# Layer 1's mixers: column tiles projected as three products of split operands, with four buffers of projected tiles

## The chip, the core and the metric

The kernel runs on one core of a Trainium2 chip. Its time is the device time of one execution in microseconds (us). A core has engines that work side by side, each on its own instructions in order: TensorE (PE; its weight loads are listed as PEld), VectorE (DVE), ScalarE (ACT), GpSimd (POOL) and SyncE (SP), whose queue issues most DMA transfers. A wait of one for another goes through semaphores.

## The reference

Two layers of a backbone with 256 latent tokens and 256 context tokens of width 1024. In each layer a modulated norm is multiplied by one input matrix, whose columns go to four mixers, and their outputs by one output matrix; then comes an expert layer. Cut to what matters here:

```python
for l in range(DEPTH):                      # DEPTH = 2
    need_ctx = l < DEPTH - 1
    h  = rms_norm(x,   norm1_g[l]) * (1 + sc1)  + sh1
    hc = rms_norm(ctx, norm1_g[l]) * (1 + csc1) + csh1
    P  = split(h  @ w_in[l]); Pc = split(hc @ w_in[l])
    y_a = conv_mixer(P[0:3]); y_b, yc_b = rwkv_mixer(P[3:9], Pc[3:9], need_ctx)
    y_c = attention(P[9:12], Pc[9:12]); y_d, yc_d = mlstm_mixer(P[12:17], Pc[12:17], need_ctx)
    x = x + gt1 * (concat(y_a, y_b, y_c, y_d) @ w_out[l])
    x = x + gt2 * peer_ffn(rms_norm(x, norm2_g[l]) * (1 + sc2) + sh2)
    if need_ctx: ...                        # the same for ctx, in layer 0 alone
```

In layer 1 the context is read but not updated: of its columns only those are wanted that feed the recurrence's state, the attention's keys and values and the mLSTM's state.

## The kernel before

Everything lies transposed: channels on the 128 partitions, the 256 tokens along the free axis. The input matrix is cut into 26 column tiles of 128; a pair of them makes one projected tile `pj` of 128 x 2 x 256. The program passes through five phases, each with its own pools of buffers: layer 0's context mixers, layer 0's latent mixers, layer 0's experts, layer 1's mixers (context first, then latents), layer 1's experts.

`mixers` (from L1070 on) is one function for all. It makes the modulated norm h (`modnorm`), and `project` then multiplies pairs of column tiles: gates and k, v, r, then the recurrence (rwkv, names rw), then keys, values and queries and the attention (at), then q, k, v, o and the mLSTM (ml), then the three tiles of the convolution (cv), and at last the output projection (wo) with the four results y. Layer 1's context takes 6 of the 13 pairs, its latents all 13. A name such as ps_p_pj1l is the PSUM bank of a projection in layer 1, latents; pj1c is layer 1, context; pj0c and wo0c are layer 0's context.

`proj` (L356) has two forms. In the native form a weight tile is loaded in halves of 128 x 512 float32 (wraw) and multiplied as it is with h (hfull): one product for each of 8 slices of the channels, which TensorE runs as two instructions. In the split form `load_split` (L333) has ScalarE copy the weights to a rounded high part (whi, type fp32r) and VectorE subtract it from the weights for a low part (wlo); h has a high and a low part likewise (hhi, hlo), and each slice takes three products: high times high, low times high, high times low. In `native` (the tuple NAT, for the phases of layer 0's context and of layer 1) it is chosen: layer 0's context phase is split, with three buffers of raw halves and two of each part (WBA = 3, 2), layer 1's phase is native, with six raw halves (WBD = 6, 0). The projected tiles have 6, 4 and 6 buffers in the three phases (PJ).

Beside them run the ada blocks: twelve for each layer, which make the modulation vectors from the conditioning; a block is eight matmuls of 32 x 512 on weights that a DMA brings each time (araw, 256 KB), a copy and four small matmuls with sel. Eight of layer 1's blocks stand in the mixers' phase of layer 1.

The order of the instructions on each engine is not written out: a scheduler makes it when the program is built, from the data's dependencies, from priorities in the order of the code, and from which buffers are free by its own estimate of times. A projected tile's buffer can be used again as soon as its last reader is done, whichever tile it was. Once built, each engine runs its list strictly in that order.

Of the kernel before, what the change touches and what calls it, by code (L numbers as in the profile page):

```python
# [24 lines left out]
DEPTH = 2  # L25
N2 = 2
YY = 6, 7, 1
NAT = False, True
HB = 1
BA = {"p": 2, "r": 3, "x": 2, "a": 1}  # L30
BD = {"p": 2, "r": 3, "x": 2, "a": 1}
ZA = "a", "a"
ZD = "a", "a"
A0 = 32
PJ = 6, 4, 6
RB = (8, 13, 4)
NW = None, None
NL = 4
LD = {"k": 2, "g": 3, "a": 1}, {"k": 3, "g": 1}
HN = 'cv', 'at', 'ml', 'rw'  # L40
WBA = 3, 2
WBD = 6, 0
XX = 7, 8, 1
CV = 0, 1, 0, 0
PA = 6, 2, 0, 0
# [179 lines left out]
class Gen:  # L225
# [1215 lines left out]
    def run(self):  # L1441
# [5 lines left out]
        with self.pool("kp") as self.kp:  # L1447
            with self.phase(MB, dict(MS, r=AR, pj=PJ[0]), {"y": "x"}, wb=WBA, native=NAT[0]) as self.ps, self.pool("wp") as self.wp:
                with self.pool("ap") as self.ap:
# [19 lines left out]
            with self.tc.using_default_side("right"):  # L1469
                self.gp = right.enter_context(self.pool("gp"))  # L1470
            with self.phase({"p": 2, "r": 4, "m": 2}, {"p": (1, 2), "r": RB, "m": (4, 3), "pj": PJ[1], "rw_gm": 4, "rw_gn": 1},
                            {"x": "r", "y": "r"}, (4, 0), True) as self.ps, self.pool("wp") as self.wp, self.pool("mp") as self.mp, self.pool("rp") as self.rp:
# [13 lines left out]
        with self.pool("kp") as self.kp:  # L1486
            with self.phase(BD, dict(MS, x=XX, y=YY, r=RR, pj=PJ[2]), {} if "y" in BD else {"y": "x"}, wb=WBD, native=NAT[1]) as self.ps, self.pool("wp") as self.wp, self.pool("mp") as self.mp:
                self.aa = *ZD, "araw"
# [65 lines left out]
```

## Time and profile before

| what | us |
| --- | --- |
| median of 3 runs | 3282.89 (3269.38 to 3284.17) |
| the profiled execution | 3267.95 |
| its span | 3266.2 |
| layer 0's context mixers in it | 40 to 357 |
| layer 0's latent mixers, with the context's expert routing | 357 to 688 |
| layer 1's mixers | 1961 to 2386 |
| layer 1's experts | from 2386 on |

The page gives busy time by engine, the chain of work that ended last, the costliest groups of instructions and the DMA issues. A TensorE instruction's span covers its way through the array, so spans of neighbours overlap: its busy time says when something was in flight, and the pitch of instructions, start to start, says how fast it works. A wait is idle time of an engine ahead of an instruction, with what ended it.

### The profile page before, as it was taken

To read this page: it belongs to the slowest core of one execution; us is meant where nothing else is said; L and a number is where in the kernel's file an instruction comes from. 1 tells how busy PE (TensorE), PEld (TensorE's weight loads), DVE (VectorE), ACT (ScalarE), POOL (GpSimd) and SP (SyncE) were. 2 spreads that over 40 slices of the span, in tenths; PEclk is the share of its full clock that TensorE was granted. 3 is DMA by queue.
4 is the path that set the end of the run, shared out by engine and by line. 5 is a ranking of instruction groups with operands and counts; after the bars stand their busy time and mean duration, and the time that the engine had idled before them with its cause. 6 is when DMAs were issued, how large, how long until landed. Compare 5 with 4: busy or idle time off the path is not lost.

```text
span 3266.2 us, 47313 instructions
## 1 busy us (share of the span) xinstructions
PE 3104.0 (95%) x18135; PEld 2630.5 (81%) x18135; DVE 2113.9 (65%) x4700; ACT 1287.7 (39%) x1752; POOL 435.3 (13%) x370
## 2 busy tenths in 40 slices
PE   7998998979989999999999999999999899999999
PEld 5576886758878989999979987867688678999998
DVE  3655476489977777777777766475368665555554
ACT  4324414235553333333333334242233554444443
POOL 0100010000014334333333320010000000000000
PEclk9899999989999999999999999999999999999999
DMA  7333412245678888887887753232344586666663
GB/s 248 123 103 121 131 51 68 84 137 197 228 284 301 295 300 283 299 294 283 283 294 284 288 196 100 69 108 74 106 166 148 223 279 210 215 205 208 213 213 129
DMA packets 278642, 640.30 MB, mean 196 GB/s; under 512 B 22672, under 2 KB 111888, under 8 KB 272912
## 3 DMA queue, kind: packets, MB, share of 16 engines
q1 hardware_dynamic: 238960, 498.66, 45.0%
q0 software_dynamic: 36864, 134.23, 11.7%
q10 hardware_dynamic: 2592, 4.39, 0.4%
q8 instruction: 142, 2.33, 0.3%
q14 instruction: 84, 0.69, 0.1%
HBM read 591.06 MB, written 46.14 MB: 195 GB/s over the span
## 4 chain that ended last, share of the span: by engine, by line
PE 72%; DVE 8%; issue 7%; ACT 6%; DMA 4%; POOL 2%; ACTq 0%; SPq 0%; DVEq 0%; POOLq 0%
PE ps_acc_ex L289 21%; PE ps_u_ex L289 19%; PE ps_a_ada L289 3%; ACT G L294 3%; PE ps_p_pj1l L289 2%; PE ps_r_rw0c L289 2%; PE ps_u_ey L289 2%; POOL ga_row L1406 2%; PE ps_p_pj0l L289 2%; PE ps_p_pj0c L289 2%; PE ps_g_gm L289 2%; PE ps_r_rw1l L289 2%; PE ps_r_rw0l L289 2%; PE ps_k_wq1l L289 2%; ACT L294 1%
## 5 line engine op out<-in xcount | busy, mean ns | idle before, releaser
L297 DVE TENSOR_TENSOR wlo<-wraw,whi 128x1024 fp32r<-128x1024 f32 (+1 forms) x560 | 648.6, 1160 | 504.7 <-ACT whi L294 502.4
L294 ACT ACTIVATE whi<-wraw 128x1024 fp32r<-128x1024 f32 (+1 forms) x560 | 563.4, 1007 | 861.2 <-PE ps_u_ex L289 452.9
L289 PE MATMUL ps_u_ex<-hhi,wlo 128*128 128x384 f32 (+1 forms) x1632 | 509.5, 312 | 0.0
L289 PE MATMUL ps_u_ex<-hhi,whi 128*128 128x384 f32 (+1 forms) x1632 | 509.0, 312 | 0.0
L289 PE MATMUL ps_u_ex<-hlo,whi 128*128 128x384 f32 (+1 forms) x1632 | 508.5, 312 | 0.0
L289 PE MATMUL ps_acc_ex<-whi,pe_ahi 128*128 128x512 f32 x1280 | 397.6, 392 | 13.0 <-ACT pe_ahi L294 13.0
L289 PE MATMUL ps_acc_ex<-wlo,pe_ahi 128*128 128x512 f32 x1280 | 397.9, 392 | 12.7 <-DVE wlo L297 12.7
L289 PE MATMUL ps_acc_ex<-whi,pe_alo 128*128 128x512 f32 x1280 | 396.9, 391 | 0.0
L289 PEld LDWEIGHTS ps_u_ex<-hhi,whi 128*128 128x128 f32 x1632 | 309.4, 190 | 5.9
L289 PEld LDWEIGHTS ps_u_ex<-hlo,whi 128*128 128x128 f32 x1632 | 309.3, 190 | 5.9
L289 PEld LDWEIGHTS ps_u_ex<-hhi,wlo 128*128 128x128 f32 x1632 | 309.2, 189 | 0.1
L289 PEld LDWEIGHTS ps_acc_ex<-wlo,pe_ahi 128*128 128x128 f32 x1280 | 240.2, 188 | 68.4 <-DVE wlo L297 16.4
L289 PEld LDWEIGHTS ps_acc_ex<-whi,pe_alo 128*128 128x128 f32 x1280 | 241.0, 188 | 52.0
L289 PEld LDWEIGHTS ps_acc_ex<-whi,pe_ahi 128*128 128x128 f32 x1280 | 236.5, 189 | 53.6 <-issue 13.3
L1406 POOL DMA_INDIRECT ga_row<-in_u,ga_i x128 | 187.6, 1466 | 409.7 <-DVE ga_a L1414 277.4
L1406 POOL DMA_INDIRECT ga_row<-in_v,ga_i x128 | 172.3, 1346 | 319.6 <-DVE ga_acc L304 291.6
L294 ACT ACTIVATE pe_ahi<-pe_a 128x384 fp32r<-128x384 f32 (+1 forms) x192 | 106.5, 556 | 235.1 <-DVE pe_a L297 163.8
L294 ACT ACTIVATE G<-ps_g_gm 128x512 f32<-128x512 f32 x160 | 158.7, 1076 | 78.9 <-PE ps_g_gm L289 78.3
L304 DVE SCALAR_TENSOR_TENSOR ga_acc<-ga_row,ga_a,ga_acc 128x1024 f32<-128x1024 f32 x127 | 163.1, 1285 | 4.3 <-DMA ga_row<-in_v,ga_i 2.3
L297 DVE TENSOR_TENSOR pe_alo<-pe_a,pe_ahi 128x384 fp32r<-128x384 f32 (+1 forms) x192 | 115.1, 600 | 77.4 <-ACT pe_ahi L294 77.3
L1414 DVE CUSTOM_DVE_ANT_0 ga_junk<-ga_row,ga_tok 128x1024 bf16<-128x1024 f32 x128 | 156.3, 1221 | 6.3 <-DMA ga_row<-in_u,ga_i 4.6
L289 PE MATMUL ps_u_ex<-hfull,xraw 128*128 128x256 f32 x576 | 143.8, 391 | 6.2 <-DVE hfull L301 6.2
(793 smaller groups left out, 4911.5 us busy)
## 6 DMA issues: line engine op xcount, KB each, us to landing
wraw<-in_v SPq DMA_DIRECT2D x256, 512.0 KB
wraw<-in_u SPq DMA_DIRECT2D x204, 512.0 KB
araw<-in_ada SPq DMA_DIRECT2D x192, 256.0 KB
wraw<-in_win SPq DMA_DIRECT2D x180, 256.0 KB
gd<-G SPq DMA_DIRECT2D x40, 1024.0 KB
xraw<-in_u SPq DMA_DIRECT2D x52, 512.0 KB
G<-gd SPq DMA_DIRECT2D x16, 1536.0 KB
wraw<-in_wq SPq DMA_DIRECT2D x32, 512.0 KB
```

What stands on the lines that cost most here:

```text
L289: self.nc.tensor.matmul(out, lhsT, rhs, start=start, stop=stop, skip_group_check=True)
L294: self.nc.scalar.activation(out, in_, func, bias=bias, scale=scale, **kw)
L297: return (eng or self.nc.vector).tensor_tensor(out=out, in0=a, in1=b, op=op)
L304: self.nc.vector.scalar_tensor_tensor(out=out, in0=a, scalar=s, in1=b, op0=op0, op1=op1)
L1406: nc.gpsimd.indirect_dma_start(out=row, out_offset=None, in_=self.I[tab], in_offset=bass.IndirectOffsetOnAxis(ap=ei[:, n : n + 1], axis=0))
L1414: nc.vector.tensor_tensor_reduce(out=junk, in0=row, in1=tok, scale=1.0, scalar=0.0, op0=ALU.mult, op1=ALU.add, accum_out=a[:, n : n + 1])
```

## The change

Three numbers change, and all for layer 1's mixers:

```diff
-NAT = False, True
+NAT = False, False
-PJ = 6, 4, 6
+PJ = 6, 4, 4
-WBD = 6, 0
+WBD = 3, 2
```

With native False, `proj` takes the split form for all column tiles and the output matrix, `parts` gives hhi and hlo in place of hfull, `modnorm` makes h in slices of 128 x 512 and splits each, and `mixers` splits y before the output projection. There are three raw halves and two of each part in place of six raw halves, and four projected tiles in place of six. The operands' bytes from memory stay the same. All that follows for the order comes from the scheduler.

TensorE at the beginning of the phase, before: ps_a_ada is an ada block, ps_p_pj1c the context's projections, ps_r_rw1c the context's recurrence.

```order
L289 MATMUL ps_p_ex_16925<-sq,ones 128x256 x8
L289 MATMUL ps_a_ada_17699<-araw,cvs 32x512 x6
L289 MATMUL ps_p_pj1c<-hfull,wraw 128x256 x48
L289 MATMUL ps_r_rw1c<-hn_sq,const 128x512
L541 MATMUL ps_r_rw1c<-const,pj_v 128x128 x4
```

And of the change, there:

```order
L289 MATMUL ps_a_ada_17856<-araw,cvs 32x512 x6
L289 MATMUL ps_p_pj1c<-hhi,whi 128x256
L289 MATMUL ps_a_ada_17856<-araw,cvs 32x512
L289 MATMUL ps_p_pj1c<-hlo,whi 128x256
L289 MATMUL ps_p_pj1c<-hhi,wlo 128x256
L289 MATMUL ps_p_pj1c<-hhi,whi 128x256
L289 MATMUL ps_p_pj1c<-hlo,whi 128x256
L289 MATMUL ps_p_pj1c<-hhi,wlo 128x256
```

Each native product has become a group of three, and the rest of the ada block, which stood behind 48 products, now stands among the first ones; until the context's recurrence starts there are 1.4 ada blocks instead of 0.5, and until that of the latents 4.4 instead of 1.4.

VectorE in the latents' recurrence, before, where the second direction's small steps (rw_row and rw_T, eight columns more at each step) alternate with the merge of the first one (rw_X) and the attention:

```order
L297 TENSOR_TENSOR rw_row_18372<-rw_row_18372,rw_M_18363 128x8x2
L820 STREAM_SHUFFLE at_sw<-at_tmp 128x256
L297 TENSOR_TENSOR rw_T_18364<-rw_T_18364,rw_row_18372 128x8x2
L297 TENSOR_TENSOR at_q<-at_tmp,exact 128x256
L700 STREAM_SHUFFLE rw_row_18372<-rw_T_18364 128x8x3
L297 TENSOR_TENSOR ps_x_at1l<-ps_x_at1l,mask 128x128
L297 TENSOR_TENSOR rw_row_18372<-rw_row_18372,rw_M_18363 128x8x3
```

And of the change, at the same steps:

```order
L297 TENSOR_TENSOR rw_row_18878<-rw_row_18878,rw_M_18869 128x8x2
L297 TENSOR_TENSOR wlo<-wraw,whi 128x512
L297 TENSOR_TENSOR rw_T_18870<-rw_T_18870,rw_row_18878 128x8x2
L297 TENSOR_TENSOR at_q<-at_q,at_sw 128x256
L700 STREAM_SHUFFLE rw_row_18878<-rw_T_18870 128x8x3
L297 TENSOR_TENSOR rw_X<-ps_r_rw1l,mask 128x16x16
L297 TENSOR_TENSOR rw_row_18878<-rw_row_18878,rw_M_18869 128x8x3
L297 TENSOR_TENSOR wlo<-wraw,whi 128x512
```

Subtractions for weights that TensorE wants later now stand between the steps. In all there are 12 of them between the first products and the last small step of the context's recurrence and 18 between the scan and the end of the latents'; the attention's query (at_q) is still made here, ahead of the merge.

TensorE at the end of the phase, before: the mLSTM's last transposes (ml_hs), two norms (hn_sq), an ada block and the output projection.

```order
L1062 MATMUL ps_x_ml1l<-const,ml_hs 128x128 x4
L289 MATMUL ps_a_ada_19835<-araw,cvs 32x512 x4
L289 MATMUL ps_x_ml1l<-hn_sq,const 128x512
L289 MATMUL ps_a_ada_19835<-araw,cvs 32x512 x4
L289 MATMUL ps_x_cv1l<-hn_sq,const 128x512
L289 MATMUL ps_a_ada_19862<-sel,araw 128x2 x4
L289 MATMUL ps_p_wo1l<-y,wraw 128x256 x64
```

And of the change:

```order
L1062 MATMUL ps_x_ml1l<-const,ml_hs 128x128 x4
L289 MATMUL ps_x_ml1l<-hn_sq,const 128x512
L289 MATMUL ps_x_cv1l<-hn_sq,const 128x512
L289 MATMUL ps_p_wo1l<-hhi,whi 128x256
L289 MATMUL ps_p_wo1l<-hlo,whi 128x256
```

The last ada block has left this place for an earlier one.

## Rows read from the trace of the kernel before

**Rows 1.** The page: busy time, share and instructions of each engine

```profile
PE 3104.0 (95%) x18135; PEld 2630.5 (81%) x18135; DVE 2113.9 (65%) x4700; ACT 1287.7 (39%) x1752; POOL 435.3 (13%) x370
```

**Rows 2.** Busy time by stretch: PE, PEld, DVE, ACT, POOL, granted clock, DMA

```profile
330.00:336.00 6.00, 6.00 (x53) 6.00 (x52) 3.55 (x6) 2.10 (x5) 0.00 (x0) 1.00 0.52 168
...
2100.00:2140.00 40.00, 39.65 (x198) 30.50 (x196) 14.16 (x35) 15.60 (x24) 1.97 (x2) 1.00 0.49 157
2140.00:2180.00 40.00, 38.30 (x209) 25.02 (x210) 32.53 (x104) 19.26 (x31) 9.16 (x8) 1.00 0.37 120
2180.00:2220.00 40.00, 39.28 (x257) 29.46 (x255) 29.62 (x129) 11.86 (x23) 3.15 (x9) 1.00 0.24 83
...
1960.00:2386.00 426.00, 406.24 (x2331) 309.15 (x2332) 224.70 (x756) 133.67 (x223) 27.84 (x41) 0.98 0.28 91
```

**Rows 3.** The chain of 1966 to 2386 us by line

```profile
by line: PE ps_p_pj1l L289 18.9%; PE ps_r_rw1l L289 14.2%; PE ps_r_rw1c L289 11.1%; PE ps_a_ada L289 8.0%; PE ps_p_pj1c L289 7.8%; PE ps_p_wo1l L289 7.2%; PE ps_x_at1l L289 4.3%; PE ps_x_ml1l L289 3.8%; DMA araw<-in_ada 3.8%; ACT L294 3.2%;
```

**Rows 4.** Waits of TensorE from 1966 to 2386 us: sum, times, longest

```profile
PE ps_a_ada L289 <- DMA araw<-in_ada: 7.2, 6, 2.8
```

**Rows 5.** Instructions by shape: busy time, mean ns, idle time before and its end

```profile
L289 PE MATMUL ps_p_pj1l<-hfull,wraw 128*128 128x256 f32 x416 | 108.5, 393 | 0.0
...
L289 PE MATMUL ps_p_pj1c<-hfull,wraw 128*128 128x256 f32 x192 | 46.9, 400 | 0.0
...
L289 PE MATMUL ps_p_wo1l<-y,wraw 128*128 128x256 f32 x128 | 30.2, 401 | 3.3 <-DVE y L304 3.3
```

**Rows 6.** The chain in order of time, layer 1: start us, us, what

```profile
2104.17 15.97 PE ps_p_pj1l L289 x74
```

**Rows 7.** The chain in order of time, layer 0's context

```profile
330.27 5.86 PE ps_p_wo0c L289 x48
```

**Rows 8.** Layer 0's context, 40 to 357 us: instructions by shape; waits of TensorE

```profile
L289 PE MATMUL ps_p_pj0c<-hhi,wlo 128*128 128x256 f32 x208 | 63.6, 306 | 3.0 <-DVE wlo L297 2.9
L289 PE MATMUL ps_p_pj0c<-hhi,whi 128*128 128x256 f32 x208 | 62.5, 301 | 9.7 <-ACT whi L294 9.7
...
L297 DVE TENSOR_TENSOR wlo<-wraw,whi 128x512 fp32r<-128x512 f32 x68 | 47.3, 700 | 42.2 <-ACT whi L294 40.5 <-PE ps_p_pj0c L289 0.8 <-DMA araw<-in_ada 0.5
L294 ACT ACTIVATE whi<-wraw 128x512 fp32r<-128x512 f32 x68 | 42.4, 628 | 65.5 <-PE ps_p_pj0c L289 45.6 <-PE ps_p_wo0c L289 12.9 <-DVE ml_H L297 2.3
...
L289 PE MATMUL ps_p_wo0c<-hhi,whi 128*128 128x256 f32 x64 | 19.3, 301 | 2.6 <-ACT hhi L294 2.6
...
PE ps_p_pj0c L289 <- ACT whi L294: 9.7, 2, 8.3
```

**Rows 9.** The chain of 36 to 360 us by line

```profile
by line: PE ps_r_rw0c L289 22.0%; PE ps_p_pj0c L289 20.2%; PE ps_a_ada L289 13.8%; PE ps_p_wo0c L289 7.7%; PE ps_x_ml0c L289 4.2%; ACT L294 4.1%; PE ps_x_at0c L289 3.3%; issue 2.3%; ACT hn_rs L294 1.6%; ACT whi L294 1.3%; DVE wlo L297 1.3%;
```

**Rows 10.** Layer 0's context, the recurrence: instructions in order of time

```profile
125.77 0.68 DVE L297 TENSOR_TENSOR wlo<-wraw,whi 128x512 fp32r<-128x512 f32 x1
...
126.51 1.78 PEld L289 LDWEIGHTS ps_r_rw0c<-rw_KR,rw_kb 64*128 64x128 f32 x9 [0.65 <-DVE wlo L297]
```

**Rows 11.** GpSimd on one tile: ns min/median/max, first and last start us

```profile
L612 POOL COPY rw_kds<-rw_kd x3: 614/700/3501, 84.3 to 2130.9; 128x512 f32<-128x512 f32 x3
```

**Rows 12.** The chain in order of time, layer 1's ada blocks

```profile
2288.32 0.97 PE ps_a_ada L289 x2
...
2341.08 1.12 PE ps_a_ada L289 x8
2343.13 4.05 DMA araw<-in_ada
```

**Rows 13.** Two projected tiles: ns min/median/max, first and last start us

```profile
L294 ACT ACTIVATE pj_aq<-ps_p_pj0l x1: 578/578/578, 510.5 to 510.5; 128x512 f32<-128x512 f32 x1
L294 ACT ACTIVATE pj_aq<-ps_p_pj1l x1: 583/583/583, 2156.7 to 2156.7; 128x512 f32<-128x512 f32 x1
...
L311 DVE COPY pj_r<-ps_p_pj0l x1: 692/692/692, 385.5 to 385.5; 128x512 f32<-128x512 f32 x1
L311 DVE COPY pj_r<-ps_p_pj1l x1: 691/691/691, 2120.2 to 2120.2; 128x512 f32<-128x512 f32 x1
```

## The prediction

> **What bounds the kernel now.** I read the page's busy times first, then the stage that the change touches by itself, then the chain that ended last within that stage. Over the whole span TensorE is busy 95% of the time, VectorE 65% and ScalarE 39% [rows 1]. Layer 1's mixers, the only stage with new code, lie between 1960 and 2386 us. There the reader should see two things: TensorE is busy 406 of 426 us, and VectorE 225, ScalarE 134, so on the face of it there is room for splitting work on the two engines beside it [rows 2]. The chain of that stage by lines says what the TensorE time is worth: pj1l 18.9%, pj1c 7.8% and wo1l 7.2%, together 33.9% of 420 us or 142 us, are the projections themselves; the recurrence (rw1l and rw1c) has 25%, the modulation blocks (ada and their DMA) nearly 12% [rows 3]. TensorE hardly waits: the largest row is 7.2 us for a DMA of the ada weights [rows 4], the largest at a projection 3.3 us for y [rows 5]. So a projection here is paid for almost in full, and whatever makes it wait for an operand would be new.
>
> **What the change removes.** A native float32 product is two TensorE instructions: 416 for pj1l, 192 for pj1c, 128 for wo1l [rows 5], so 208 + 96 + 64 = 368 products. Their pitch, where they run without a break, is 15.97 us for 74 instructions, 0.2158 us each and 0.4316 us for a product [rows 6]. Layer 0's context mixers already run the new form: 48 split products in 5.86 us, 0.1221 us each, 0.366 us for the three that replace one [rows 7]. The saving is 0.0656 x 368 = 24.1 us of TensorE time. The chain has 142 us of the 368 x 0.4316 = 158.8 us, so I count 0.89 of it: **-21.5 us**. [...]
>
> **What it adds on the other engines.** 23 pairs of column tiles (6 for the context, 13 for the latents, 4 for the output projection) make 92 half tiles, each with one ScalarE copy of 0.628 us and one VectorE subtraction of 0.700 us [rows 8]; the two norms and y make 12 more pairs of splits of the same size. That is 104 x 0.70 = 73 us on VectorE and 104 x 0.63 = 65 us on ScalarE. The average leaves room for both (225 + 73 = 298 of 426). Part of it lies beside projections that run in a row: from 2100 to 2140 VectorE is busy 14 of 40 us [rows 2].
>
> **Waits of TensorE for its operands.** This is the term that the trace before doesn't show for layer 1, and shows for layer 0. In the same form, with the same three raw and two split buffers, pj0c waited 9.7 us for whi and 3.0 us for wlo, wo0c 2.6 us for hhi [rows 8]: 15.3 us for 13 + 4 = 17 pairs, 0.90 us a pair. For 23 pairs that is **+20.7 us**. The lower bound is 0 (everything prefetched). The upper is 32 us, if the 8.4 us that whi and wlo have in layer 0's chain (1.3% and 1.3% of 324 us [rows 9]) come on top, at 23/17 of that; but these two views overlap, so I stay with the row of the same form, 20.7.
>
> **VectorE's and ScalarE's queues.** In the recurrence VectorE sets the pace: it is busy 62 of the 80 us from 2140 to 2220 [rows 2]. The instruction order puts 12 subtractions into the context's recurrence and 18 into the latents', with 4 of the latents' norm among the context's merge; behind each, on an engine that works in order, stand the recurrence's small operations, and TensorE waits for these. Layer 0 shows the picture: a subtraction of 0.68 us among the steps, and behind it the recurrence's next weight load 0.65 us late, with that subtraction as what ended the wait [rows 10]. In full, 34 x 0.70 = 24 us; none, if all fall into gaps. Most of layer 0's subtractions waited for ScalarE's copy rather than held anything up (42 us of idle time ahead of 47 us [rows 8]), so I take 0.3 of it, **+7 us**, and keep 0 and 24.
>
> **GpSimd.** Its copy rw_kds took 3.50 us in layer 0's context stage, among the splits, and 0.70 and 0.61 us in the two stages without them [rows 11]. At most 2.9 us, then, and nothing where the result is wanted late: **+1 us**. [...]
>
> **Modulation blocks and buffers.** The eight ada blocks stay, but stand elsewhere: a run of one or of four of their matmuls (two instructions each) costs about 1 us either way (2288.32 and 2341.08 [rows 12]), and the order has 28 such runs where it had 31: **-3 us**. The last block leaves the tail, where its runs and a DMA of 4.05 us stand ahead of the output projection (2341.08 and 2343.13 [rows 12]); it goes to stretches where a block costs as much, so I count that at nothing, between -7 and +6 us. What would be late next at that place is y: its split, 0.63 + 0.70 us, which the term for waits contains. Four projected tiles instead of six: the order still has the attention's keys and queries ahead of the recurrence's merge, since k and the gate tile fall free when the second direction is prepared. So 0, and the other case is a rival. Three raw and two split buffers hold five half tiles instead of six; the projections never waited for a weight DMA (0.0 us ahead of pj1l and pj1c [rows 5]), 0 again.
>
> **Sum.** -21.5 + 20.7 + 7 + 1 - 3 = +4.2 us, 3272 us on the profiled execution's own 3267.95 us (span 3266.2). That execution is 15 us under the median of the three runs shown (3282.89; 3269.38 to 3284.17); the same 4.2 us on the median give **3287 us**.
>
> **Rivals.**
> - *The waits are hidden.* Layer 0's 15.3 us were few and long (8.3 of whi's 9.7 us in one piece [rows 8]), and layer 1 could escape them. Then the waits cost 5 us and the queues none: -21.5 + 5 - 3 = -19.5, 3263 us. For it: VectorE's slack of 53% on average. Against: layer 1 runs the same code in the same order of engines.
> - *VectorE becomes the bound of the recurrence.* All 34 subtractions at full price, GpSimd at its upper bound: -21.5 + 20.7 + 24 + 2.9 - 3 = +23.1, and 3306 us. It decides from the point where VectorE is busy in 2140 to 2220 for more than 90% instead of 78%; 9 half tiles there would do (6.3 us on 62). For it: layer 0 shows one that is waited for [rows 10]. Against: many of them stand behind copies out of PSUM, where the engine waits anyway.
> - *The four buffers hold the attention back*, so that part of the change undoes the other. Layer 0's latents have four: there pj_aq was written 125 us after pj_r (510.5 and 385.5), in layer 1 with six 36 us after (2156.7 and 2120.2) [rows 13]. If so here, the attention's 4.3% of 420 us, 18 us, come behind the recurrence: 3305 us. Against it stands the order, as told.
>
> **How the numbers follow.** What can be told from no change here is about 0.5%, 16 us. The forecast, with both terms near each other: 0.50. Waits hidden: 0.20. VectorE bound: 0.26. Buffers: 0.04. Faster by more than 0.5% is the first rival, 0.20; slower the other two, 0.30; the rest, 0.50, within. The forecast alone spans 3273 to 3301 us (waits and queues, 28 us together, between half and one and a half of their size). The range reaches a little past both rivals' times: 3259 us (no waits, no queueing, -24) to 3313 us (+23.1, and some 6 us for an ada block at a bad place).
>
> **What would show it.** Right: three rows of 208 + 96 + 64 products at a pitch of 0.12 us; idle time of TensorE before pj1c, pj1l and wo1l, ended by whi, wlo and hhi, of some 20 us in place of none; VectorE busy near 298 us in the stage; the stage as long as before within 10 us. Wrong: the stage shorter by 20 us with idle time of few us before those matmuls (the first rival), or the time from pj_r to the last recurrence row longer than before with VectorE above 90% (the second), or pj_aq behind the recurrence (the third). A split product slower than 0.122 us in this stage would break the first term.

## The result, and the profile after

The changed kernel took 3312.63 us (median of five, 3303.65 to 3317.96) beside 3279.4 us for the kernel before (five, 3269.38 to 3284.17): a ratio on record of **1.0116**, 95% interval 1.009 to 1.0142, 30 to 47 us slower (the two medians alone give 1.0101). I had forecast 4 us and given "slower" three chances in ten. One execution below, of e8_ghost6, took 7164.72 us and is left out of its ratio. The profiled execution after has a span of 3310.8 us, 44.6 more than the profiled one before, which is 11 us under its median; 41.2 of them lie ahead of the first matmul behind layer 1's output projection (2385.3 us before, 2426.5 after).

First the stretches after: busy time of PE, PEld, DVE, ACT and POOL, granted TensorE clock, DMA share, GB/s.

```profile
1966.00:2426.00 460.00, 412.78 (x2676) 334.82 (x2672) 287.52 (x847) 186.12 (x316) 31.63 (x41) 0.86 0.27 85
...
2000.00:2010.00 10.00, 6.70 (x46) 4.99 (x45) 6.92 (x17) 7.72 (x13) 0.00 (x0) 0.86 0.30 81
2010.00:2030.00 20.00, 20.00 (x86) 17.17 (x86) 9.36 (x24) 6.88 (x11) 3.89 (x3) 0.50 0.30 92
2195.00:2235.00 40.00, 38.45 (x176) 34.97 (x175) 18.97 (x74) 6.59 (x10) 4.98 (x10) 0.54 0.04 14
2365.00:2400.00 35.00, 16.37 (x60) 10.74 (x59) 15.75 (x44) 13.94 (x17) 1.77 (x2) 0.50 0.00 0
...
2140.00:2220.00 80.00, 70.24 (x376) 53.97 (x375) 57.60 (x170) 37.96 (x60) 15.98 (x15) 0.78 0.24 75
```

Read the last column but two. The granted clock of the stage is 0.86; before it was 0.98 [rows 2]. It isn't a little lower everywhere: in three stretches of 20 to 40 us it stands at 0.50 to 0.54; no row of 5 us of the traces before and after reads under 0.50. In the first two TensorE is busy nearly throughout (20.0 of 20 and 38.5 of 40 us), and works at that clock. VectorE, which I feared, is busy less of 2140 to 2220 than before, 57.6 of 80 us; 20 us later, where the recurrence has come as far as before, it is 54.9.

What TensorE waits for (sum, times, longest), 1966 to 2426 us, answers to [rows 4]:

```profile
PE ps_a_ada L289 <- DMA araw<-in_ada: 8.4, 5, 2.7
PE ps_p_wo1l L289 <- ACT hhi L294: 5.2, 1, 5.2
PE ps_x_cv1l L289 <- ACT hn_sq L294: 5.2, 1, 5.2
PE ps_a_ada L289 <- ACT araw L294: 5.0, 5, 2.0
PE ps_p_pj1c L289 <- DVE wlo L297: 3.8, 3, 3.3
PE ps_x_ml1l L289 <- DVE ml_W L297: 3.3, 1, 3.3
...
PE ps_p_pj1l L289 <- DVE wlo L297: 1.7, 2, 1.1
```

The groups by shape (busy, mean ns, idle time before and its end) answer to [rows 5] and [rows 8]: the products and splits are there as foreseen.

```profile
L289 PE MATMUL ps_p_pj1l<-hhi,whi 128*128 128x256 f32 x208 | 63.4, 305 | 1.3 <-ACT whi L294 1.1 <-ACT hhi L294 0.3
L289 PE MATMUL ps_p_pj1l<-hhi,wlo 128*128 128x256 f32 x208 | 63.4, 305 | 1.7 <-DVE wlo L297 1.7
L297 DVE TENSOR_TENSOR wlo<-wraw,whi 128x512 fp32r<-128x512 f32 x90 | 62.6, 697 | 38.1 <-ACT whi L294 36.7 <-PE ps_p_pj1l L289 1.1
...
L294 ACT ACTIVATE whi<-wraw 128x512 fp32r<-128x512 f32 x90 | 56.4, 630 | 130.8 <-PE ps_p_pj1l L289 65.0 <-PE ps_p_pj1c L289 21.1 <-PE ps_p_wo1l L289 12.8
...
L289 PE MATMUL ps_p_pj1c<-hhi,wlo 128*128 128x256 f32 x96 | 30.4, 317 | 3.8 <-DVE wlo L297 3.8
...
L289 PE MATMUL ps_p_wo1l<-hhi,whi 128*128 128x256 f32 x64 | 19.2, 299 | 5.2 <-ACT hhi L294 5.2
```

What a fall looks like: TensorE's instructions in order of time around 2008 us (start, duration, operands, idle time before).

```profile
2003.62 0.28 PE L289 MATMUL ps_p_pj1c<-hhi,whi 128*128 128x256 f32 x1
2003.74 0.28 PE L289 MATMUL ps_p_pj1c<-hlo,whi 128*128 128x256 f32 x1
...
2005.28 0.28 PE L289 MATMUL ps_p_pj1c<-hlo,whi 128*128 128x256 f32 x1
2008.86 0.58 PE L289 MATMUL ps_p_pj1c<-hhi,wlo 128*128 128x256 f32 x1 [3.30 <-DVE wlo L297]
...
2010.95 0.41 PE L289 MATMUL ps_p_pj1c<-hhi,wlo 128*128 128x256 f32 x1
2011.16 0.41 PE L289 MATMUL ps_p_pj1c<-hhi,whi 128*128 128x256 f32 x1
```

The starts lie 0.12 us apart until TensorE stands 3.3 us for a low half, and 0.21 us apart behind it. Three such products take 0.64 us, where one native product at full clock takes 0.43 [rows 6].

Where the 41.2 us lie, by the first and last matmuls of each part: +20.0 until the latents' recurrence begins (2120.0 before, 2140.0 after), +11.9 in it (146.1 and 158.0 us), +13.0 from its end to the output projection (87.9 and 100.9), -3.7 in that. Each of the first three holds one of the three slow stretches.

### The profile page after: what moved, and what is told of

Read it like the earlier page. It is cut to its first block, busy times and chain, and to the rows that moved or that the text cites. A ratio compares the mean times of both kernels' runs of the same rounds, so it can differ in the third digit from the quotient of the medians.

```text
span 3310.8 us, 48402 instructions
## 1 busy us (share of the span) xinstructions
PE 3116.9 (94%) x18503; PEld 2661.6 (80%) x18503; DVE 2178.9 (66%) x4804; ACT 1345.2 (41%) x1854; POOL 439.5 (13%) x370
## 5 line engine op out<-in xcount | busy, mean ns | idle before, releaser
L297 DVE TENSOR_TENSOR wlo<-wraw,whi 128x1024 fp32r<-128x1024 f32 (+1 forms) x652 | 711.7, 1093 | 547.0 <-ACT whi L294 543.2
L294 ACT ACTIVATE whi<-wraw 128x1024 fp32r<-128x1024 f32 (+1 forms) x652 | 621.0, 954 | 1002.1 <-PE ps_u_ex L289 454.8
```

What stands on the lines that cost most here:

```text
L294: self.nc.scalar.activation(out, in_, func, bias=bias, scale=scale, **kw)
L297: return (eng or self.nc.vector).tensor_tensor(out=out, in0=a, in1=b, op=op)
```

## The experiments

Each ran in three rounds beside the kernel before on the same chip. "Low" and "idle" are summed from full rows of 5 us between 1965 us and the first matmul behind the output projection ("end"): low is twice what the granted clock lacks of 1, in us, so that a us at 0.50 counts as one, idle what TensorE's busy time lacks of 5 us. The ratio is of all executions; end, low and idle are of the profiled one. (The 129 and 24 us of low clock in the expectations count from 1960 to 2430.)

| run | ratio, interval | end | low | idle |
|---|---|---|---|---|
| before | | 2385.3 | 15 | 18 |
| after | 1.0116 (1.009-1.0142) | 2426.5 | 126 | 47 |
| e1_pj4 | 0.9995 (0.9974-1.0016) | 2382.0 | 31 | 17 |
| e7_raw3 | 1.0016 (1.000-1.0033) | 2398.2 | 38 | 22 |
| e8_ghost6 | 1.0041 (1.0017-1.0064) | 2397.3 | 34 | 28 |
| e2_ghost | 1.0166 (1.013-1.0202) | 2438.2 | 99 | 34 |
| e4_fixed | 1.0033 (1.0013-1.0054) | 2397.0 | 61 | 46 |
| e5_ctx_split | 1.0044 (1.0028-1.0059) | 2405.1 | 72 | 27 |
| e6_lat_split | 1.0059 (1.0032-1.0086) | 2415.5 | 92 | 35 |
| e3_four | 1.0139 (1.0114-1.0164) | 2435.7 | 65 | 29 |
| g3_slots | 1.0098 (1.0066-1.013) | 2421.4 | 130 | 43 |
| f1_raw5 | 1.0115 (1.007-1.0159) | 2417.5 | 122 | 43 |
| f2_pairs3 | 1.0191 (1.0124-1.0258) | 2483.7 | 239 | 47 |
| f3_raw2 | 1.0193 (1.0121-1.0265) | 2442.6 | 147 | 56 |
| f4_gpsimd | 1.0192 (1.0145-1.024) | 2470.7 | 177 | 58 |

### The parts of the change

**e1_pj4**, the buffers of projected tiles alone:

```
-PJ = 6, 4, 6
+PJ = 6, 4, 4
```

> Native products as before, with four buffers of projected tiles instead of six; nothing else of the change. Clock theory (the loss comes from TensorE standing and its granted clock falling in layer 1's mixers, 129 us at the low level after the change and 24 before) and queue theory (the split instructions themselves hold up ScalarE and VectorE): no split here, so the time is that of before, ratio 0.997 to 1.003, low level about 24 us in 1960 to 2430. Buffers theory (four buffers hold the projections and with them the attention back): ratio 1.006 or more, 20 to 40 us slower, pj_aq more than 36 us behind pj_r.

No loss. pj_aq now stood 53 us behind pj_r (2167.3 and 2114.3; 36 before), and it cost nothing. The third rival of the prediction is out.

**e2_ghost**, native products beside splits that nothing reads (e1 and `WBD = 3, 2`):

```
             self.nc.sync.dma_start(raw, src)
+            if self.l1:
+                hi = self.t(pool, shape, tag + "hi", F32R, n[1])
+                lo = self.t(pool, shape, tag + "lo", F32R, n[1])
+                self.split(raw, hi, lo)
             return raw, None
```

> Native products with four projected buffers, three raw buffers and two pairs of halves as in the changed kernel: each weight tile of layer 1 is also split, but no product reads the halves (the split of the normalized input is left out). It puts the weights' 104 conversions and 104 subtractions into the queues of ScalarE and VectorE without TensorE ever waiting for one. Clock theory: TensorE does as much as before and waits little, low level under 50 us in 1960 to 2430, ratio to before 0.998 to 1.005 (at most 15 us for the queues). Queue theory: most of the loss is here too, ratio 1.007 to 1.015, 25 to 45 us, with the stretch from pj_r to wo1l as long as in the changed kernel (259 us; before 234).

(The weights have 92 half tiles; 104, here and in f4_gpsimd's expectation, counts the norms and y too.) The queue theory's number, and more. But not as a queue would do it: TensorE, with native work, idles only 16 us more than before, and its clock is low for 84 us more.

```profile
1966.00:2438.00 472.00, 437.16 (x2311) 330.30 (x2304) 279.71 (x834) 181.74 (x307) 30.00 (x41) 0.90 0.27 84
```

**e7_raw3** (e1 and `WBD = 3, 0`) and **e8_ghost6** (e2 and `WBD = 6, 2`) take that run apart.

> Native products, four projected buffers, and three raw weight buffers in place of six; nothing is split. Theory of the raw buffers (the loads run three half tiles ahead at most, and that is what cost the run with unread halves 55 us): ratio to before 1.006 to 1.016, 20 to 50 us, with waits of TensorE for wraw of some us and more low clock than 38 us. Theory of the queues (the conversions and subtractions hold up ScalarE and VectorE): no loss here, 0.997 to 1.003, low clock 25 to 45 us in 1960 to 2430.

> As the run with unread halves (native products, each weight tile of layer 1 also split, the halves read by nothing), but with six raw buffers and two pairs of halves, so that the loads run as far ahead as before. Theory of the queues: the loss stays, ratio 1.010 to 1.018, 33 to 60 us, low clock 80 us or more. Theory of the raw buffers: it goes, 0.998 to 1.004.

```profile
1966.00:2397.00 431.00, 403.19 (x2304) 305.71 (x2304) 275.37 (x831) 177.88 (x301) 31.31 (x41) 0.96 0.28 89
```

Neither theory by itself: three raw buffers cost about 5 us (the queue theory's band), the splits in the queues 13 us (just over the band of the raw buffers), both together 54. The same work with the same splits ends 41 us earlier when six raw buffers feed it, and the rows differ in the clock (0.96 and 0.90) far more than in idle time.

**e5_ctx_split** and **e6_lat_split** set, for layer 1, `self.native = g == "l"` and `self.native = g == "c"` at the head of `mixers` (the native input shares hlo's buffer).

> The changed kernel with split products for the contexts of layer 1 alone (96 products), native ones for the latents (272); buffers as in the changed kernel, three raw. The changed kernel lay 20 us behind before when the latents' pj_r was written and 45 us when wo1l began. Theory of the queues: what the contexts lose stays (15 to 22 us), the rest goes: ratio 1.004 to 1.007. Theory of the raw buffers: the latents lose with native products too, 1.009 or more.

> The changed kernel with native products for the contexts of layer 1 (96) and split ones for the latents (272). Theory of the queues: the contexts' 20 us go and the latents' 25 us stay, ratio 1.006 to 1.010, with the stretch from pj_r to wo1l near the changed kernel's 259 us. Theory of the raw buffers: contexts and latents lose as in the changed kernel or more, 1.010 to 1.016.

14 and 19 us, near the queue theory's forecasts (the second just under its band) and, together, 33 of the change's 38. The loss is in no single place.

**e4_fixed** takes the waits for weight halves away:

```
+                if self.l1:
+                    fix = hlo[:, k, 0:P]
+                    self.mm(out, fix, hhi[:, k, :n], start=first)
+                    self.mm(out, fix, hlo[:, k, :n])
+                    self.mm(out, fix, hhi[:, k, :n], stop=last)
+                    continue
```

> The changed kernel with layer 1's three products reading the low half of the input as their weights in place of the halves of the weight tiles (other data, and the weights' share of the result is left out): weight tiles are loaded and split as before, but TensorE never waits for a half of a weight tile. Clock theory: without these waits the idle time falls by some 10 to 20 us, the low level from 129 us to under 60, and the time to the sum without waits, 15 to 25 us under the kernel before, ratio 0.992 to 0.996. Queue theory: the splits stand in the queues all the same, ratio 1.004 to 1.012 and a recurrence as long as in the changed kernel.

It lies between the two: 27 of the 38 us come back and 65 us of low clock go, but idle time stays at 46 us, and it doesn't get below the kernel before. Most of the loss goes with the waits for weight halves; they are not all of what makes TensorE stand. What is left of low clock lies in one place: 41 of 61 us between 2332 and 2375 us, ahead of the output projection.

### The clock

**e3_four** adds a product (`wlo` by `hlo`) to the three.

> The changed kernel with a fourth product, low half by low half, in layer 1's mixers: 368 more TensorE instructions, at the pitch of 0.122 us 45 us of work at full clock. Clock theory: the added work stands where TensorE stood or ran at half clock, so the low level falls from 129 us to under 90 and the time rises by much less than 45 us: 0 to 20 us above the changed kernel, 3300 to 3335. Queue theory: the recurrence waits for VectorE and hides the work there, but not in the projections ahead of it; the clock stays as it is, 20 to 35 us above the changed kernel.

45 us of work added, and the stage ends 9.2 us later: low falls from 126 to 65, idle from 47 to 29. Both came out as the clock theory had it.

**g3_slots** (`XX = 7, 7, 1`, `RR = (3, 13, 4)`) is the control of **f1_raw5** (it and `WBD = 5, 2`) and **f2_pairs3** (it and `WBD = 3, 3`); **f3_raw2** has `WBD = 2, 2`.

> The changed kernel with five raw weight buffers and two pairs of halves instead of three and two (room from one work tile less in each of the attention's and the recurrence's pools). Theory of the chain of few buffers (a raw tile is given back only when ScalarE and VectorE have come to its two split instructions in their queues, so with three the next loads start late and TensorE stands): low clock from 129 us to 60 to 90, ratio to before 0.999 to 1.006, against 1.0116 for the change. Rival, the queues by themselves (the two instructions delay the recurrence's own): no change against the changed kernel, 1.009 to 1.014.

> The changed kernel with three raw buffers and three pairs of halves instead of two (room as in the run with five raw). Theory of the chain of few buffers: the splits may run one half tile further ahead of TensorE, low clock 70 to 100 us, ratio 1.002 to 1.008. Rival, the queues by themselves: 1.009 to 1.014. If raw buffers alone are short and not pairs: also 1.009 to 1.014, and the run with five raw below it.

> The changed kernel with two raw buffers instead of three. Theory of the chain of few buffers: worse by some 20 to 60 us, ratio 1.018 to 1.030, low clock 160 us or more. Rival, the queues by themselves: as the changed kernel, 1.009 to 1.014.

> The changed kernel with one work tile less in the attention's and in the recurrence's pool, as in the runs with five raw buffers and three pairs, and nothing else: the control of those two. If the order alone moves the falls of the clock about: anywhere from 1.008 to 1.022, with low clock between 100 and 240 us and idle time near the changed kernel's 47 us. If the slots change nothing: 1.010 to 1.013, low clock 115 to 140 us.

My theory of too few buffers got no support from f1 and f2: five raw buffers change nothing (f1 against g3), and a third pair of halves, forecast to help, gives the higher median (the intervals of f2 and g3 overlap a little). With two raw buffers, f3, the ratio is the theory's and the low clock is under its 160 us; its interval too overlaps the change's. g3 doesn't tell its own two cases apart.

f2's profile is the clearest on the clock. It idles as long as the changed kernel, 47 us, has the same instructions in another order, and ends 57.2 us later; its low clock is 113 us longer, half of which is 56.5.

```profile
1966.00:2483.00 517.00, 470.19 (x2672) 380.53 (x2672) 286.29 (x845) 184.14 (x314) 29.09 (x41) 0.77 0.24 75
2205.00:2260.00 55.00, 54.03 (x201) 40.91 (x202) 26.45 (x99) 8.24 (x13) 6.02 (x10) 0.50 0.08 25
2090.00:2125.00 35.00, 35.00 (x170) 34.32 (x170) 8.94 (x26) 3.34 (x6) 0.00 (x0) 0.50 0.05 16
```

That execution is the slowest of f2's four, though (3322.3 to 3367.42 us, granted clock of the whole span 0.961 to 0.946), so the new order alone is not worth 57 us. The repeated executions are a test of their own, since in them the program and its order are the same. The kernel before took 3260 to 3289 us in the 74 executions beside these runs, at 0.982 to 0.970: 118 to 197 us of low clock over the whole span, with 0.34 us of time for each us of it by a straight line (correlation 0.94). So time goes with the clock in one and the same program, though this alone doesn't tell which of the two moves the other; and a difference of a few tens of us of low clock between two profiles says little by itself.

A time at low clock in which TensorE stands is counted in the table under both heads. Take instead, in each row of 5 us, what the clock lacks of 1 times TensorE's busy time: 50 us after and 6 before. What is left of the end without idle time and this I take as work at full clock. That is an estimate, which counts speed in proportion to the granted clock; the pitch of the products above went from 0.12 to 0.21 us, less than twice. It is 2330 (after), 2324 (g3), 2325 (f1), 2331 (f2), 2328 (f3) and 2337 (f4, below) in the kernels with the same split products, 2353 to 2363 in the native ones (before, e1, e2, e7, e8), and 2377 in e3, 48 over the changed kernel for 45 us of work added.

**f4_gpsimd** does the subtraction with `nc.gpsimd.tensor_tensor`.

> The changed kernel with the 104 subtractions of layer 1's weight tiles on GpSimd instead of VectorE (28 us busy there in the stage before). Theory of the queues: VectorE's queue is free of them, so the time falls if VectorE is the culprit: ratio 1.002 to 1.008. If ScalarE's conversion is what comes late, or a subtraction takes much longer on GpSimd: as the changed kernel or slower, 1.010 to 1.020.

```profile
L349 POOL TENSOR_TENSOR wlo<-wraw,whi 128x512 fp32r<-128x512 f32 x90 | 120.4, 1340 | 289.6 <-ACT whi L294 275.7 <-PE ps_p_pj1l L289 10.4 <-DMA wraw<-in_win 2.5
```

The case of the long subtraction came in: 1.34 us there and 0.70 on VectorE. What a free queue of VectorE is worth by itself is not shown, since the halves come later; f4 says only that it is worth less than the later halves cost.

### What sets off a fall

**g1_no_ada** and **g2_nat_no_ada** put `NL = 12` for `NL = 4`, in the changed kernel and in the one before.

> The changed kernel with all twelve of layer 1's modulation blocks before the experts of layer 0, so that none of the eight that stood in layer 1's mixers is left there (they cost TensorE the same elsewhere, some 6 us each). If the blocks' waits for their transfers and for ScalarE set off the falls of the clock: low clock in the stage from 126 us to under 60, ratio to the kernel before 0.996 to 1.004. If the waits for the split halves do: low clock stays over 100 us, ratio 1.008 to 1.015. The blocks also fill gaps; if that counts more, it gets slower, over 1.015.

> The kernel before (native products) with the same move of the modulation blocks. If the blocks' waits matter for the split products alone: 0.998 to 1.003, low clock near 15 us. If they fill gaps that native products leave: slower, 1.003 to 1.010. If their waits cost here too: faster, 0.992 to 0.998.

Ratios 1.0422 (1.0393-1.0452) and 1.0278 (1.0243-1.0313): the stage starts 100 and 96 us later, so the blocks cost far more ahead of the experts than I had put down, and the ratios of the blocks' and the halves' case missed. The comparison holds: without any block in the stage, split against native is 3408.55 to 3357.87 us, 51 us, more than with them, and the clock of both stages is lower than with the blocks (0.81 and 0.92, first changed, then native; the first makes 174 us of low clock, over the 100 of g1's second case). The blocks' waits are not what does it. Their work, by the expectation some 6 us a block for eight of them, is gone from the stages, and yet these are only 1 and 9 us shorter than with them (459 and 460, 410 and 419): the blocks fill gaps.

```profile
2066.00:2525.00 459.00, 393.76 (x2488) 341.97 (x2488) 286.66 (x837) 180.94 (x309) 32.31 (x41) 0.81 0.17 51
```

```profile
2062.00:2472.00 410.00, 370.86 (x2120) 304.69 (x2120) 221.61 (x735) 124.24 (x209) 28.41 (x41) 0.92 0.18 56
```

**g4_l0_native** (`NAT = True, True`, `WBA = 6, 0` on the kernel before):

> The kernel before with native products in layer 0's contexts too (split there before, 40 to 357 us) and six raw buffers, none split. If split products cost clock wherever they stand among a recurrence: the low clock of 0 to 400 us falls by 30 us or more and the idle time with it, which pays for some 24 us more of products: ratio 0.990 to 1.001. If the stage there is bound otherwise (loads of 256 KB per half tile, short stages): 1.002 to 1.008, the products' longer time.

1.0043 (1.0024-1.0063), slower, as the second case had it: low clock in 0 to 400 us is 47.8 us with either, idle falls from 39.0 to 28.3, and the longer products cost more than that. So split products don't cost clock wherever they stand.

**h1_fill** and **h2_nat_fill** add, behind steps of the latents' recurrence and mLSTM, useless products on the step's operands:

```
+            ps = self.bank("p")
+            for j in range(2):
+                self.mm(ps[:, 0 : rhs.shape[-1]], lhsT, rhs, start=True, stop=True)
```

> The changed kernel with two useless native products (128 columns by 256, their result is read by nothing) behind each of 44 steps of the latents' recurrence and mLSTM in layer 1, on that step's own operands: 88 products of 0.43 us, 38 us more work for TensorE at full clock. If the half clock itself is what costs: the falls in the recurrence (2195 to 2237) go, low clock from 126 us to under 80, and the added work costs far less than it takes: ratio to the kernel before 1.006 to 1.015, 0 to 10 us above the changed kernel at most. If the low clock only goes along with waits: the work comes on top or fills them without a change of clock: 1.018 to 1.024, low clock over 110 us.

> The same 88 useless products in the kernel before, whose clock is up in that stretch already: nothing to win back, so 25 to 38 us slower by either reading, ratio 1.007 to 1.012. Under 1.004 it would say that the products fit into gaps of TensorE that have nothing to do with the clock.

1.031 (1.0278-1.0342) and 1.0269 (1.0239-1.0299). Both totals lie over every band, with 150 us of low clock (over the 110 of h1's second case) and 79 of idle time in h1, 103 and 48 in h2. They decide nothing: the added products take turns with the projections in the same two PSUM banks and push those back (pj_aq 2293.0 and 2278.4). In the recurrence alone, behind its first 60 us, there is something to read in h1:

```profile
2195.00:2280.00 85.00, 82.21 (x597) 73.53 (x597) 36.09 (x130) 10.79 (x19) 2.14 (x8) 1.00 0.00 1
```

Where the changed kernel ran at 0.50 the clock is 1.00, with two more products behind each step. But in the 62 us ahead of that it is 0.75, and in h2 it is 0.78 in the recurrence's first 61 us, where the kernel before has 1.00 throughout. The recurrence takes 147.1 us in h1, 158.0 after, 147.3 in h2 and 146.1 before, and h1 and h2 lack the projections that stood in it. So h1 doesn't price the clock.

**The third stretch.** For this one the runs show what goes with the fall. These are the last 40 us ahead of the output projection, in the kernel before, after, in e3_four, in g2_nat_no_ada and in e4_fixed:

```profile
2314.00:2354.00 40.00, 34.41 (x193) 23.00 (x192) 19.77 (x64) 13.88 (x17) 1.78 (x2) 0.97 0.28 92
2358.90:2398.90 40.00, 20.55 (x84) 14.17 (x85) 18.40 (x57) 14.98 (x19) 1.77 (x2) 0.54 0.02 7
2361.60:2401.60 40.00, 33.51 (x212) 23.44 (x210) 24.17 (x65) 20.16 (x28) 1.87 (x2) 0.96 0.25 79
2401.30:2441.30 40.00, 22.89 (x110) 15.88 (x109) 18.98 (x61) 12.68 (x15) 1.77 (x2) 0.62 0.04 14
2330.60:2370.60 40.00, 19.94 (x83) 13.52 (x82) 20.24 (x59) 14.03 (x18) 1.77 (x2) 0.55 0.01 2
```

Before and in e3, the last projection starts 14 and 15 us ahead of the output projection, among mLSTM's last steps, and an ada block follows. After, the last one starts 42 us ahead and no ada block is there; mLSTM's steps stand alone, and TensorE waits between them. g2 has native products and no split, but its last projection starts 36 us ahead and there is no block either, and it shows the same waits and the same fall. The longest of mLSTM's, after and then in g2:

```profile
2368.80 2.03 PE L289 MATMUL ps_x_ml1l<-ml_va,ml_W 128*128 128x65 f32 x8 [3.29 <-DVE ml_W L297]
2413.17 2.04 PE L289 MATMUL ps_x_ml1l<-ml_va,ml_W 128*128 128x65 f32 x8 [3.55 <-DVE ml_W L297]
```

The same holds over the other runs without useless products: where the last projection starts 15 us ahead or less, the clock of these 40 us is 0.82 to 0.98 (before, e3, e5, g4); where it starts 34 us ahead or more, 0.50 to 0.62 (after, e4, f1, f2, f4, g1, g2, g3); in between it is 0.54 to 0.92 (e1, e2, e6, e7, e8, f3). So the third fall goes with other work running out under mLSTM, in native and split kernels alike, and not with waits for split weights, which e4 hasn't got.

**The first two.** In e4, without waits for weight halves, 20 us of low clock are left ahead of the third stretch, where the changed kernel has some 85. The first fall begins behind the wait of 3.30 us for a low half, shown above. The second doesn't begin behind a long wait: from 2186 to 2198 us, just ahead of it, TensorE works at full clock and no wait is over 0.5 us.

```profile
2186.00:2198.00 12.00, 10.18 (x61) 7.32 (x61) 11.01 (x30) 3.79 (x6) 2.82 (x3) 1.00 0.22 82
```

## Why the prediction was wrong

- **The step that failed is the first one.** Both pitches come from stretches with a granted clock of 1.00 (330 to 336 and 2100 to 2140 us [rows 2]), and the sum then held that clock for all 368 products and for everything between them. The clock had no term; it was put at nothing without a reason. The stage's low clock went from 15 to 126 us, and what it costs while TensorE is busy from 6 to 50 us.
- **The saving itself was there**: 0.12 us a product at full clock. Work at full clock, as taken above, is 32 us less, against 24.1 + 3 forecast.
- **Waits and queues**: I had +20.7, +7 and +1, 28.7 us. TensorE's idle time rose by 29 us, but not as I had shared it out: 12.3 us were waits for whi, wlo and hhi (1.1, 0.3, 1.7, 3.8, 5.2, 0.2 in the groups above) in place of 3.3 for y; the ada blocks' waits are 5.7 us longer, those of mLSTM 9.5 and those of the convolution 5.2. The total agrees by luck. GpSimd was busy 31.63 us instead of 27.84, and no wait of TensorE there names it.
- **Modulation blocks**: "The last block leaves the tail" I counted at nothing, between -7 and +6 us. In the tail's 40 us TensorE idles 14 us more than before, nearly half of the 29, and runs at 0.54. The block is one part of it; the projections, which end earlier, are the other.
- **Sum**: 29 of idle time and 44 for the clock against -32 of work make the 41 us. It closes because work is what is left over; what speaks for it is that work comes out nearly the same in all kernels with the same products.
- **The range** reached to 3313 us, for VectorE's queue and an ada block, and the time lies just inside it. That is luck.
- **Of what was to show it right**, the three rows of 208, 96 and 64 products at 0.12 us (at full clock) are there, VectorE has 287.5 us for the 298 expected, and the stage is 41 us longer instead of 10 at most.
- **VectorE as the bound** had the time nearly right (3306) and the reason wrong: its condition was 90% busy in 2140 to 2220, and it was 72%. I had also misread two numbers: 53% is VectorE's busy share and not its slack, and 9 half tiles on 62 us make 85% of 80 us; 90% would take 14. The buffers cost nothing, as argued.
- Layer 0's context mixers, my model for the waits, stand at 0.94 over 0 to 400 us in the trace before. I had read their waits and not their clock. In the trace after, the first stretch begins at such a wait: products 0.12 us apart ahead of 3.3 us of waiting for a low half, 0.21 us apart behind it.

**What stays open.** That the low clock makes the difference in length is shown by f2's profile against the changed kernel's, by e3 and by the repeated executions. What goes with the third fall is shown by e3 and g2. What sets off the first two is less clear: weight halves have the largest part (e4), unread splits do it too when raw buffers are few (e2 against e8), yet more raw buffers don't mend the change (f1). The order of the instructions differs in each of these kernels, and no pair of them held it fixed. No version beat the kernel before; e1_pj4 equals it with 4 KB less per partition.

## What to carry to other kernels

Cheaper instructions on an engine that is hardly ever idle (18 us of the stage here) can shorten the cover that it gives to everything around, as in the third stretch here, where the last projection starts 42 us ahead of the output projection and no longer 14: before counting on them, ask what TensorE will do in the gaps that open, and price the work behind each gap at a low clock too (0.50 here, 0.21 us a product for 0.12). Compare the granted clock of every stretch before comparing waits: two profiles with equal idle time here differed by 57 us with it, and executions of one program by 29. A useful sum for a stage is work at full clock, plus idle time, plus half of the time that TensorE is busy at a clock of 0.50.

## What the hardware showed that I had not expected

The clock stayed low under an engine that the trace shows as busy. From 2200 to 2235 us after, TensorE was busy 34.3 of 35 us, at 0.50 throughout. The groups of 2195 to 2235, first after, then before:

```profile
L289 PE MATMUL ps_r_rw1l<-rw_T,rw_gm 128*128 128x64 f32 x48 | 11.0, 412 | 0.0
L289 PE MATMUL ps_r_rw1l<-rw_Tt,rw_X 128*128 128x64 f32 (+1 forms) x41 | 8.8, 397 | 0.0
L289 PE MATMUL ps_r_rw1l<-rw_X,rw_Tt 128*128 128x64 f32 x32 | 7.6, 419 | 0.0
L289 PE MATMUL ps_p_pj1l<-hhi,wlo 128*128 128x256 f32 x7 | 3.2, 457 | 0.0
```

```profile
L289 PE MATMUL ps_p_pj1l<-hfull,wraw 128*128 128x256 f32 x36 | 10.2, 402 | 0.0
L289 PE MATMUL ps_r_rw1l<-rw_T,rw_gm 128*128 128x64 f32 x63 | 8.1, 271 | 0.0
L289 PE MATMUL ps_r_rw1l<-rw_Tt,rw_X 128*128 128x64 f32 (+1 forms) x56 | 6.4, 261 | 0.0
```

After, these are mostly the recurrence's dependent matmuls of 64 columns, with 21 split products between them; before, the clock was 1.00 there and in the whole recurrence, with 36 matmuls of native products in the mixture, and also 14 matmuls of an ada block and some 30 of the attention. In h1, with two useless products behind each step, it was 1.00. Which part of the mixture does it, no run separates. 34.3 us of busy time did not bring the clock back: a busy TensorE in a profile does not tell that its clock is up.
